# Down projection: all weight sums by accumulating DMA, neighbouring k tiles paired, products reordered, last norms without GpSimd

## The chip, the cores and the metric

The kernel runs on one core of one Trainium2 chip. The metric is the time of one execution on the device in microseconds (us); the median of the runs is compared. Each core has TensorE (PE, matmuls), VectorE (DVE), ScalarE (ACT), GpSimd (POOL) and SyncE (SP, which here only starts transfers), and 16 DMA engines that move data. Each engine works through its own list of instructions in order and waits at semaphores for the others.

## The reference

One encoder layer over two groups of 256 tokens, 1024 channels wide, all in fp32. The part that matters here is the gated feed-forward network at its end, and the norm behind it:

```python
def conv_ffn(x, w_ffn_up, ffn_conv_w, ffn_conv_b, w_ffn_down):
    u = dwconv_centred(x @ w_ffn_up, ffn_conv_w, ffn_conv_b)
    return (jax.nn.gelu(u[..., :D_FF]) * u[..., D_FF:]) @ w_ffn_down
...
    x = layer_norm(DEEPNORM_ALPHA * x + mixed, ln1_g[l], ln1_b[l])
    ff = conv_ffn(x, w_ffn_up[l], ffn_conv_w[l], ffn_conv_b[l], w_ffn_down[l])
    x = layer_norm(DEEPNORM_ALPHA * x + ff, ln2_g[l], ln2_b[l])
```

`D_FF` is 2816, so the product with `w_ffn_down` has 22 k tiles of 128 rows. Its input has 512 rows (4 tiles of 128) and its output 1024 columns (2 halves of 512): 8 output tiles (t, half), each in a PSUM bank of its own.

## The kernel before

Every fp32 matmul is made of three float32r matmuls: each operand is split into a high part (a rounding cast, on ACT) and a low part (a subtraction, on DVE), and high by high, high by low and low by high are added up in PSUM.

The down projection has two parts. The first 8 k tiles are multiplied plainly: `down(f)` for f = 0 to 7 gives 24 matmuls each (L1147 to L1149). The other 14 k tiles form 7 pairs i. For each pair the two k tiles, each cut into a left and a right half of columns, are a 2x2 block matrix `raw[i, r, c]` (tiles named `b...`, 128x512), and the pair's input is a 2x2 block matrix A(i, r, c) of 128x256 blocks. In place of 8 block products the Strassen-Winograd scheme makes 7, on sums of blocks. Product p over all pairs is 7 x 2 x 3 = 42 matmuls (`part`, L1268 to L1270), added up in a pair of banks.

The sums of input blocks (s1 to s4, 128x256) and of weight blocks (t1 to t4, 128x512) are made shortly before or after a product's operands are split. s1 to s4, t1 and t2 are subtractions or additions on DVE (L1168 to L1183). t3 and t4 are `late_sum`: ACT negates the destination (L1187), then a DMA that POOL starts adds the source to it on its way (L1188); POOL itself is occupied only with issuing.

`prepare` makes the split operands (`wop` for weights, `xop` for inputs: cast on ACT in L1222, low part on DVE in L1223), six steps (p, i) ahead of the matmuls. `PRODUCTS` lists for each product the sums to be made before its operands, the operands, the sums to be made after it, and which weight blocks are then free. Its order is the order of work: 1, 5, 6, 3, 7, 2, 4. In the whole program a Tile scheduler decides which order the instructions of an engine finally have.

After the plain part, DVE reads all 8 banks into the residual `y[t][half]` (`residual`, L1052), and the products start the banks anew. Product 2 has banks of its own, product 4 goes on upon the banks of product 7. Each `add_to` (L1262) adds a finished bank to y.

At the end every tile of y is normalised and stored. `layer_norm(..., share=True)` does the first half on DVE (L308, L316) and the second on ACT and GpSimd: ACT standardises it (L324), GpSimd multiplies and adds the gains (L334, L335). The reciprocal root of the variance is a small GpSimd operation (L115) in any case. Row tiles 0 and 1 are normalised while product 4 runs; the last tile is done without sharing, in three pieces.

The weight blocks come by 28 loads of 256 KB each, started by SP (L1156), into slots that are shared with other tiles (62 slots in all); a load waits until its slot is free.

Of the kernel before, what the change touches and what calls it, by code (L numbers as in the profile page):

```python
# [29 lines left out]
NF = DFF // P  # L30
# [13 lines left out]
NP = 7  # L44
# [4 lines left out]
class Encoder:  # L49
# [759 lines left out]
    def build(self):  # L809
        nc, io = self.nc, self.io  # L810
# [51 lines left out]
        with self.tc.manual_schedule(engines=engines):  # L862
# [30 lines left out]
            ps = self.ps("lncol")  # L893
# [138 lines left out]
        y = {}  # L1032
# [18 lines left out]
        def residual(t, h, ps):  # L1051
            nc.vector.scalar_tensor_tensor(y[t][h], y[t][h], ALPHA, ps, op0=ALU.mult, op1=ALU.add)  # L1052
# [27 lines left out]

        hf, hs, up = {}, {}, {}

        def ev_up(f, which):
# [12 lines left out]

# [37 lines left out]

        w_dn = io["w_ffn_down"][0]
        acc = {}
        PL = NF - 2 * NP
        raw, sums, ops = {}, {}, {}
        mm = nc.tensor.matmul
        tt = nc.vector.tensor_tensor  # L1140

        def down_mm(f, t, half, wh, wl):
            down_split(f)
# [6 lines left out]

        def load_pair(i):
            for r in range(2):
                k = PL + r * NP + i
# [4 lines left out]
        def A(i, r, c):  # L1158
            return hf[PL + c * NP + i][:, r * T : r * T + T]

        def S(i):
            if i % 2 == 0 and i // 2 not in sums:
                sums[i // 2] = self.a("ssum")
            return sums[i // 2][:, (i % 2) * T : (i % 2) * T + T]


        def sum_s1(i):
            tt(S(i), A(i, 1, 0), A(i, 1, 1), op=ALU.add)  # L1168

        def sum_s2(i):  # L1170
            tt(S(i), S(i), A(i, 0, 0), op=ALU.subtract)

        def sum_s3(i):
            tt(A(i, 1, 0), A(i, 0, 0), A(i, 1, 0), op=ALU.subtract)
# [22 lines left out]
        PRODUCTS = {  # L1197
            1: ((), lambda i: A(i, 0, 0), lambda i: raw[i, 0, 0], (sum_t1, sum_s1, sum_s3), ()),
            5: ((), S, lambda i: raw[i, 0, 0], (sum_t3,), ()),
            6: ((sum_t2, sum_s2), S, lambda i: raw[i, 0, 0], (sum_t4,), ()),  # L1200
            3: ((sum_s4,), S, lambda i: raw[i, 1, 1], (), ((1, 1),)),
            7: ((), lambda i: A(i, 1, 0), lambda i: raw[i, 0, 1], (), ((0, 1),)),
            2: ((), lambda i: A(i, 0, 1), lambda i: raw[i, 1, 0], (), ((1, 0),)),
            4: ((), lambda i: A(i, 1, 1), lambda i: raw[i, 0, 0], (), ((0, 0),)),
        }
        steps = [(p, i) for p in PRODUCTS for i in range(NP)]
# [3 lines left out]
        def prepare(n):  # L1210
            while len(made) < min(n, len(steps)):
                p, i = next(ahead)
                before, x, w, later, done = PRODUCTS[p]
                for f in before:
                    f(i)
                o = []
                wsrc, xsrc = w(i), x(i)
                wt = self.whl.tile([P, 1024], F32R, tag=("hi", "lo")[len(made) % 2], name="wop")
                xt = self.a("xop", F32R)
                for z, src, n_ in ((wt, wsrc, 512), (xt, xsrc, T)):  # L1220
                    h, l = z[:, :n_], z[:, n_ : 2 * n_]
                    nc.scalar.copy(h, src)  # L1222
                    tt(l, src, h.bitcast(F32), op=ALU.subtract)  # L1223
                    o += [h, l]
                ops[p, i] = o
                for f in later:
                    f(i)
                for r, c in done:
                    del raw[i, r, c]
                if p == 3 and i % 2 == 1 or p == 3 and i == NP - 1:  # L1230
                    del sums[i // 2]
                if p == 7:
                    del hf[PL + i]
                if p == 4:
                    del hf[PL + NP + i]
                made.append((p, i))

        dn = [self.chunk(w_dn, f, 1, 0, D) for f in range(PL)]

        def down(f):  # L1240
            def run():
                if f == 0:
                    for t in range(NTT):
                        for half in range(2):
                            acc[t, half] = self.ps(f"dn{t}{half}", dense=(t >= 2))
                for z in range(f, min(f + 3, PL)):
                    down_split(z)
                wh, wl = dn[f].get()
                for t in range(NTT):
                    for half in range(2):  # L1250
                        down_mm(f, t, half, wh, wl)
# [7 lines left out]
            return run  # L1259

        def add_to(t, half, ps):
            tt(y[t][half], y[t][half], ps, op=ALU.add)  # L1262

        def part(p, i, j, out, first, c=slice(0, 512)):
            wh, wl, xh, xl = ops[p, i]
# [6 lines left out]
        def product(p, bank, first, sinks):  # L1272


            def run():
                n = list(PRODUCTS).index(p) * NP
                for i in range(NP):
                    prepare(n + i + 1 + STEPS)
                    for j in range(2):
                        part(p, i, j, acc[bank[0] + 2 * j, bank[1]], first)  # L1280
                    del ops[p, i]
                for r, c in sinks:
                    for j in range(2):
                        add_to(2 * r + j, c, acc[bank[0] + 2 * j, bank[1]])
            return run

        BA, BB, BC, BD = (0, 0), (1, 0), (0, 1), (1, 1)

        def store(t, h, c=slice(0, 512)):
            nc.sync.dma_start(  # L1290
# [1 line left out]
                y[t][h][:, c],  # L1292
            )

        def tail():
            gb2 = self.gains(io["ln2_g"], io["ln2_b"])
            prepare(len(steps))
            for t in range(2):
                self.layer_norm(y[t], gb2, None, True)
                for h in range(2):  # L1300
                    store(t, h)

            o = acc[BA[0], BA[1]]
            for i in range(NP):
                part(4, i, 0, o, False)
            add_to(2, 0, o)
            self.layer_norm(y[2], gb2, None, True)
            for h in range(2):
                store(2, h)
            st = self.sm([P, 4, 6], "lnst4")  # L1310
            z = y[3]
            for n in range(2):
                c = slice(n * 256, n * 256 + 256)
                nc.vector.bn_stats(st[:, n, :], z[1][:, c])
            for n, bank in enumerate((BC, BD)):
                c = slice(n * 256, n * 256 + 256)
                o = acc[bank][:, c]
# [5 lines left out]
            self.layer_norm(z, gb2, st, False, pieces, lambda h, c: store(3, h, c))  # L1323
# [6 lines left out]
        self.add(product(3, BB, False, [(0, 1)]))  # L1330
        self.add(product(7, BA, False, [(1, 1)]))
        self.add(product(2, BC, True, [(0, 0)]))

        self.add(lambda: add_to(3, 0, acc[BA[0] + 2, BA[1]]))
        self.add(tail)
        self.run_jobs()

# [75 lines left out]
```

## Time and profile before

| | before |
|---|---|
| runs (3) | 945.25 us median, 944.57 to 946.96 |
| the profiled execution | 946.11 us, its span 944.3 us, TensorE clock 0.994 |
| PE busy over the span | 927.4 us (98%) |
| DVE busy | 605.3 us (64%) |
| ACT busy | 407.6 us (43%) |
| POOL busy | 106.5 us (11%) |
| plain part of the down projection | first matmul at 821.21 us, last at 864.50 |
| seven products | 864.73 to 931.8 us |
| last operation of DVE ends | 940.99 us |

Busy time counts work and no waiting. The span is the time from the first to the last instruction; the execution takes 1.81 us more than it. A duration in a row includes the pipeline's fill; the distance of two starts in a row without a wait is what an instruction costs its engine. A note in square brackets at the end of a row is idle time before it and what ended that.

### The profile page before, as it was taken

What the parts mean: (1) busy time and instruction counts of PE and PEld (TensorE: products, weight loads), DVE (VectorE), ACT (ScalarE), POOL (GpSimd) and SP (SyncE); (2) the same over time, 40 slices, a digit from 0 to 9 for tenths busy, and PEclk for the clock granted to TensorE, in tenths of its full rate; (3) what the DMA queues carried; (4) which work ended last, traced back from release to release, by engine and by line L of the source; (5) the groups of instructions that cost most, each with busy time, mean ns of one, the idle gap of its engine ahead of it and who ended that gap; (6) DMA issues with size and microseconds to landing.
All of it is one profiled execution on the core that took longest, in us unless ns stands there. A gap on an engine that the chain in (4) does not pass through costs nothing.

```text
span 944.3 us, 12395 instructions
## 1 busy us (share of the span) xinstructions
PE 927.4 (98%) x4633; PEld 789.3 (84%) x4633; DVE 605.3 (64%) x1145; ACT 407.6 (43%) x761; POOL 106.5 (11%) x105
## 2 busy tenths in 40 slices
PE   8999999999999999999999999999999999999994
PEld 6888888888889998888888889988888888888884
DVE  4584444896777535367667758755555555677997
ACT  4562543434555435344336312533343343454861
POOL 0100100450000000121007401000000000011205
PEclk9999999999999999999999999999999999999998
DMA  8354223224111243433245433333333332473412
GB/s 290 89 161 144 75 68 90 73 62 131 53 46 44 66 136 89 142 96 98 68 123 173 152 89 89 104 98 90 105 96 89 105 96 90 165 228 87 79 45 89
DMA packets 125663, 99.44 MB, mean 105 GB/s; under 512 B 4128, under 2 KB 106532, under 8 KB 125604
## 3 DMA queue, kind: packets, MB, share of 16 engines
q1 hardware_dynamic: 123588, 94.99, 33.2%
q0 software_dynamic: 2016, 3.67, 2.3%
q8 instruction: 36, 0.59, 0.3%
q14 instruction: 23, 0.19, 0.1%
HBM read 92.86 MB, written 2.11 MB: 101 GB/s over the span
## 4 chain that ended last, share of the span: by engine, by line
PE 92%; DVE 3%; POOL 2%; DMA 1%; ACT 1%; issue 0%; POOLq 0%; DVEq 0%; SPq 0%; ACTq 0%
PE ua L122 4%; PE ub L123 4%; PE ub L122 4%; PE ua L123 4%; PE ua L124 4%; PE ub L124 4%; PE vc L837 3%; PE dn L1270 2%; PE dn L1268 2%; PE dn L1269 2%; PE ga L122 2%; PE vog L171 2%; PE vog L172 2%; PE vog L170 2%; PE ga L123 2%; PE ba L122 2%
## 5 line engine op out<-in xcount | busy, mean ns | idle before, releaser
L111 DVE TENSOR_TENSOR wlo<-raw,whi 128x1024 fp32r<-128x1024 f32 (+3 forms) x148 | 176.7, 1198 | 217.2 <-ACT whi L110 217.0
L110 ACT CAST whi<-raw 128x1024 fp32r<-128x1024 f32 (+3 forms) x148 | 148.2, 1009 | 295.7 <-PE ua L123 72.0
L1188 POOL DMA_DIRECT2D b<-b x14 | 12.4, 905 | 293.2 <-ACT xop L1222 270.1
L1270 PE MATMUL dn<-wop,xop 128*128 128x512 f32 (+1 forms) x105 | 39.4, 375 | 0.0
L1269 PE MATMUL dn<-wop,xop 128*128 128x512 f32 (+1 forms) x105 | 39.4, 375 | 0.0
L1268 PE MATMUL dn<-wop,xop 128*128 128x512 f32 (+1 forms) x105 | 39.4, 375 | 0.0
L1223 DVE TENSOR_TENSOR wop<-b,wop 128x512 fp32r<-128x512 f32 x49 | 33.7, 699 | 4.5 <-ACT wop L1222 4.5
L1222 ACT CAST wop<-b 128x512 fp32r<-128x512 f32 x49 | 29.5, 619 | 15.7 <-PE dn L1148 6.0
L405 ACT ACTIVATE prob<-sc,nmax 128x256 f32<-128x256 f32 x48 | 22.4, 475 | 24.7 <-DVE nmax L401 24.6
L1089 ACT ACTIVATE up<-up 128x512 f32<-128x512 f32 x22 | 13.9, 633 | 42.5 <-DVE up L476 42.4
L115 POOL TENSOR_TENSOR rss<-rss,mhalf 128x4 f32<-128x4 f32 (+1 forms) x12 | 22.6, 1884 | 75.5 <-DVE rss L784 75.5
L1269 PEld LDWEIGHTS dn<-wop,xop 128*128 128x128 f32 x105 | 19.8, 188 | 3.6
L1270 PEld LDWEIGHTS dn<-wop,xop 128*128 128x128 f32 x105 | 19.8, 188 | 3.6
L1268 PEld LDWEIGHTS dn<-wop,xop 128*128 128x128 f32 x105 | 19.8, 188 | 3.5
L334 POOL TENSOR_TENSOR y<-y,gain 128x512 f32<-128x512 f32 x11 | 18.4, 1680 | 20.1 <-PE gm L123 19.0
L401 DVE TENSOR_REDUCE nmax<-sc 128x2 f32<-128x512 f32 x24 | 16.4, 683 | 4.3 <-PE sc L124 4.3
L335 POOL TENSOR_TENSOR y<-y,gain 128x512 f32<-128x512 f32 x11 | 18.8, 1716 | 0.5
L115 POOL TENSOR_TENSOR lnmv<-lnmv,mhalf 128x1 f32<-128x1 f32 x8 | 7.7, 959 | 86.9 <-DVE lnmv L297 86.9
L85 DVE TENSOR_TENSOR probTl<-pt,probTh 128x512 fp32r<-128x512 f32 x24 | 16.4, 684 | 1.4 <-ACT probTh L84 1.4
L473 DVE SCALAR_TENSOR_TENSOR up<-ub,col,up 128x510 f32<-128x510 f32 x20 | 14.9, 744 | 2.7 <-ACT up L470 2.7
L996 DVE SCALAR_TENSOR_TENSOR gate<-gate,ba 128x512 f32<-128x512 f32 x8 | 5.5, 686 | 17.1 <-PE ba L124 9.2
L470 ACT ACTIVATE up<-ub,col 128x512 f32<-128x512 f32 x20 | 15.5, 775 | 1.2 <-PE ub L124 1.2
(1371 smaller groups left out, 2933.6 us busy)
## 6 DMA issues: line engine op xcount, KB each, us to landing
raw<-in_w_in SPq DMA_DIRECT2D x48, 512.0 KB
raw<-in_w_ffn_up SPq DMA_DIRECT2D x44, 512.0 KB
b<-in_w_ffn_down SPq DMA_DIRECT2D x28, 256.0 KB
raw<-in_w_mem_kv SPq DMA_DIRECT2D x8, 512.0 KB
raw<-in_w_branch_attn SPq DMA_DIRECT2D x8, 512.0 KB
raw<-in_w_out SPq DMA_DIRECT2D x8, 512.0 KB
raw<-in_w_ffn_down SPq DMA_DIRECT2D x8, 512.0 KB
b<-b POOLq DMA_DIRECT2D x14, 256.0 KB, 3.6
```

The costliest lines, as they stand in the source:

```text
L110: nc.scalar.copy(hi[:, s], raw[:, s])
L111: nc.vector.tensor_tensor(lo[:, s], raw[:, s], hi[:, s].bitcast(F32), op=ALU.subtract)
L115: self.nc.gpsimd.tensor_tensor(out, in_, self.mhalf.to_broadcast(list(in_.shape)), op=ALU.pow)
L122: mm(ps, lh, rh, start=first, stop=False)
L123: mm(ps, lh, rl, start=False, stop=False)
L124: mm(ps, ll, rh, start=False, stop=last)
L837: nc.tensor.matmul(vps[t], memT[2 * c + kk][xi][:, ts], w[wi][:, kk, :], start=(c + kk + xi + wi == 0), stop=(wi == 1 and 2 * c + kk == KT ...
L1222: nc.scalar.copy(h, src)
L1223: tt(l, src, h.bitcast(F32), op=ALU.subtract)
L1268: mm(out, xh[:, ts], wh[:, c], start=first and i == 0, stop=False, skip_group_check=go_on)
L1269: mm(out, xh[:, ts], wl[:, c], start=False, stop=False, skip_group_check=go_on)
L1270: mm(out, xl[:, ts], wh[:, c], start=False, stop=i == NP - 1, skip_group_check=go_on)
```

## The change

- t1 and t2 are made as t3 and t4 are: a negation on ACT and an accumulating DMA from POOL. There are 28 such sums where there were 14.
- A pair is two neighbouring k tiles (8+2i, 9+2i) and no longer tiles 7 apart (8+i, 15+i). s1 and s3 of a pair are made as soon as its second hidden tile is there, in the up projection.
- The products' order is 1, 5, 2, 6, 3, 7, 4. Product 2 goes on upon banks of the plain part; product 4 goes on upon one of the two banks of product 7 and needs new starts for the other output tile only.
- Of the 8 residual reads 4 come after the plain part; the other 4 output tiles get theirs with the first bank that a product adds to them. Within a k tile of the plain part the order of the output tiles is another.
- The last norms share nothing with ACT and GpSimd: both halves are done on DVE. `finish` normalises and stores row tile 0 in product 7 and row tile 1 ahead of product 4; the gains are loaded in product 3.

```diff
         def ev_up(f, which):
...
                 nc.vector.tensor_tensor(hf[f], up[f], u, op=ALU.mult)
+                if f >= PL and (f - PL) % 2:
+                    sum_s1((f - PL) // 2)
+                    sum_s3((f - PL) // 2)
...
-        def sum_t1(i):
-            tt(raw[i, 0, 0], raw[i, 0, 1], raw[i, 0, 0], op=ALU.subtract)
-
-        def sum_t2(i):
-            tt(raw[i, 0, 0], raw[i, 1, 1], raw[i, 0, 0], op=ALU.subtract)
...
+        def sum_t1(i):
+            late_sum(raw[i, 0, 0], raw[i, 0, 1])
+
+        def sum_t2(i):
+            late_sum(raw[i, 0, 0], raw[i, 1, 1])
...
-            1: ((), lambda i: A(i, 0, 0), lambda i: raw[i, 0, 0], (sum_t1, sum_s1, sum_s3), ()),
-            5: ((), S, lambda i: raw[i, 0, 0], (sum_t3,), ()),
-            6: ((sum_t2, sum_s2), S, lambda i: raw[i, 0, 0], (sum_t4,), ()),
+            1: ((), lambda i: A(i, 0, 0), lambda i: raw[i, 0, 0], (sum_t1,), ()),
+            5: ((), S, lambda i: raw[i, 0, 0], (sum_t2, sum_t3), ()),
+            2: ((), lambda i: A(i, 0, 1), lambda i: raw[i, 1, 0], (), ()),
+            6: ((sum_s2,), S, lambda i: raw[i, 0, 0], (sum_t4,), ((1, 0),)),
...
-                        if f == PL - 1:
-                            residual(t, half, acc[t, half])
+                for t, half in ((0, 1), (1, 1), (2, 0), (3, 0), (0, 0), (1, 0), (2, 1), (3, 1)):
+                    down_mm(f, t, half, wh, wl)
+                    if f == PL - 1 and half != t // 2:
+                        add_to(t, half, acc[t, half])
...
+        BA, BB = [acc_of(0, 1), acc_of(1, 1)], [acc_of(2, 0), acc_of(3, 0)]
+        BC, BD = [acc_of(0, 0), acc_of(1, 0)], [acc_of(2, 1), acc_of(3, 1)]
...
+                    if between and i == NP // 2:
+                        between()
...
+        def finish(t, st=None):
+            self.layer_norm(y[t], y["gb2"], st)
+            for h in range(2):
+                store(t, h)
...
-            for t in range(2):
-                self.layer_norm(y[t], gb2, None, True)
...
+            finish(1)
+
+            add_to(3, 0, BA[1]())
+            o = BA[0]()
             for i in range(NP):
                 part(4, i, 0, o, False)
...
+        self.add(product(2, BC, False, [(0, 0)]))
+        self.add(lambda: read(BD, 1, 1))
+        self.add(product(6, BA, False, [(0, 1)]))
+        self.add(product(3, BB, False, [(0, 1)], lambda: y.update(gb2=self.gains(io["ln2_g"], io["ln2_b"]))))
+        self.add(product(7, BA, False, [(1, 1)], lambda: finish(0)))
         self.add(tail)
```

How the lists of the engines change is shown at three places. The weight blocks of one pair carry four numbers; before, those of pair 0 are b_7269, b_7271, b_7273, b_7275 (left upper, right upper, left lower, right lower), now b_7287, b_7289, b_7291, b_7293; pair 1 begins at b_7311 before and b_7329 now, pair 2 at b_7363 and b_7379.

The first place is the plain part, on ACT: the casts of operands (L1222, now L1227), the splits of hidden tiles for the plain matmuls (L84), of plain weights (L110), and the negations (L1187, now L1186). ACT before:

```order
L1222 CAST wop<-b_7311 128x512
L84 CAST hs4h<-hf_5976 128x512
L110 CAST whi<-raw 128x1024
L1187 ACTIVATE b_7313<-b_7313 128x512
L1222 CAST xop<-hf_6341 128x256
L84 CAST hs5h<-hf_6049 128x512
L1222 CAST xop<-hf_6414 128x256
```

ACT now:

```order
L1227 CAST wop<-b_7329 128x512
L1186 ACTIVATE b_7289<-b_7289 128x512
L1186 ACTIVATE b_7329<-b_7329 128x512
L110 CAST whi<-raw 128x1024
L1227 CAST xop<-hf_6417 128x256
L84 CAST hs5h<-hf_6049 128x512
L1186 ACTIVATE b_7331<-b_7331 128x512
L1227 CAST wop<-b_7379 128x512
L1227 CAST xop<-hf_6565 128x256
L84 CAST hs6h<-hf_6122 128x512
L1186 ACTIVATE b_7379<-b_7379 128x512
```

The negation of a pair's right upper block (b_7289, b_7331) must wait until the accumulating DMA that reads it (into b_7287, b_7329) has landed, and the negation of the next pair's left upper block stands behind it.

POOL's accumulating DMAs in the same place, destination and source, before:

```order
L1188 DMA b_7271<-b_7275 128x512
L1188 DMA b_7313<-b_7317 128x512
L1188 DMA b_7365<-b_7369 128x512
L1188 DMA b_7416<-b_7420 128x512
L1188 DMA b_7513<-b_7517 128x512
```

And now:

```order
L1187 DMA b_7287<-b_7289 128x512
L1187 DMA b_7289<-b_7293 128x512
L1187 DMA b_7329<-b_7331 128x512
L1187 DMA b_7331<-b_7335 128x512
L1187 DMA b_7379<-b_7381 128x512
L1187 DMA b_7381<-b_7385 128x512
L1187 DMA b_7429<-b_7431 128x512
L1187 DMA b_7431<-b_7435 128x512
L1187 DMA b_7479<-b_7481 128x512
L1187 DMA b_7523<-b_7525 128x512
L1187 DMA b_7481<-b_7485 128x512
L1187 DMA b_7287<-b_7293 128x512
```

t1 and t3 alternate pair by pair, and t2 (the last row) follows among them; before, only t3 stood here.

The second place is DVE at the end of the plain part: the low parts of operands (L1223, now L1228) and the residual reads (L1052). DVE before:

```order
L1223 TENSOR_TENSOR wop<-b_7553,wop 128x512
L1183 TENSOR_TENSOR b_7269<-b_7275,b_7269 128x512
L1180 TENSOR_TENSOR b_7553<-b_7555,b_7553 128x512
L1223 TENSOR_TENSOR xop<-hf_6633,xop 128x256
L1223 TENSOR_TENSOR xop<-hf_6706,xop 128x256
L1052 SCALAR_TENSOR_TENSOR y_4767<-y_4767,dn_7237 128x512
```

DVE now:

```order
L1228 TENSOR_TENSOR wop<-b_7287,wop 128x512
L1228 TENSOR_TENSOR wop<-b_7563,wop 128x512
L1228 TENSOR_TENSOR wop<-b_7379,wop 128x512
L1228 TENSOR_TENSOR xop<-hf_7011,xop 128x256
L1052 SCALAR_TENSOR_TENSOR y_4768<-y_4768,dn_7256 128x512
L1052 SCALAR_TENSOR_TENSOR y_4778<-y_4778,dn_7258 128x512
L1052 SCALAR_TENSOR_TENSOR y_4787<-y_4787,dn_7259 128x512
L1052 SCALAR_TENSOR_TENSOR y_4797<-y_4797,dn_7261 128x512
L1228 TENSOR_TENSOR wop<-b_7329,wop 128x512
L1228 TENSOR_TENSOR xop<-hf_7153,xop 128x256
```

The input operand of the first product's last pair (hf_7153) stands behind four residual reads; on ACT its cast stands behind the negation of b_7565, which waits for the landing of the last t1.

The third place is DVE at the end: `add_to` (L1262, now L1272), the statistics (L294) and the two halves of the norm's last steps (L308, L316), y_4767 and y_4768 being the halves of row tile 0, y_4777 and y_4778 of tile 1, y_4787 and y_4788 of tile 2, y_4797 and y_4798 of tile 3. DVE before:

```order
L1262 TENSOR_TENSOR y_4767<-y_4767,dn_7238 128x512
L1262 TENSOR_TENSOR y_4777<-y_4777,dn_7242 128x512
L294 BN_STATS lnst<-y_4767 128x6
L294 BN_STATS lnst<-y_4777 128x6
L296 BN_AGGR lnmv<-lnst 128x2
L294 BN_STATS lnst<-y_4778 128x6
L297 TENSOR_SCALAR lnmv<-lnmv 128x1
L308 SCALAR_TENSOR_TENSOR y_4767<-y_4767,lnmv,gain 128x512
L327 SCALAR_TENSOR_TENSOR lnmv<-lnmv 128x1
```

DVE now:

```order
L1228 TENSOR_TENSOR wop<-b_7563,wop 128x512
L1228 TENSOR_TENSOR xop<-hf_7244,xop 128x256
L294 BN_STATS lnst<-y_4777 128x6
L294 BN_STATS lnst<-y_4778 128x6
L1272 TENSOR_TENSOR y_4788<-y_4788,dn_7256 128x512
L1272 TENSOR_TENSOR y_4798<-y_4798,dn_7258 128x512
L296 BN_AGGR lnmv<-lnst 128x2
L1272 TENSOR_TENSOR y_4797<-y_4797,dn_7258 128x512
L297 TENSOR_SCALAR lnmv<-lnmv 128x1
L308 SCALAR_TENSOR_TENSOR y_4777<-y_4777,lnmv,gain 128x512
L308 SCALAR_TENSOR_TENSOR y_4778<-y_4778,lnmv,gain 128x512
```

Before, two norms stand in a row after the last operands; now row tile 0 is finished between the operands, and the reads of product 7's banks (dn_7256, dn_7258) stand here, upon the first of which product 4 goes on.

## Rows read from the trace of the kernel before

**Rows 1.** The page: DVE's busy tenths in 40 slices of the span.

```profile
DVE  4584444896777535367667758755555555677997
```

**Rows 2.** Windows: stretch, length, busy PE, PEld, DVE, ACT, POOL, PEclk, DMA share, GB/s.

```profile
877.00:885.00 8.00, 8.00 (x37) 6.64 (x36) 8.00 (x18) 7.12 (x15) 3.62 (x5) 1.00 0.59 100
```

**Rows 3.** Timeline of PE (start, duration): the products' first and last matmul.

```profile
864.73 0.39 PE L1268 MATMUL dn<-wop,xop 128*128 128x512 f32 x1
...
931.52 0.28 PE L1270 MATMUL dn<-wop,xop 128*128 128x256 f32 x1
```

**Rows 4.** Timeline of DVE, end of the plain part and end of the program.

```profile
859.70 0.76 DVE L1223 TENSOR_TENSOR xop<-hf,xop 128x256 fp32r<-128x256 f32 x2 [2.73 <-ACT xop L1222]
860.38 5.24 DVE L1052 SCALAR_TENSOR_TENSOR y<-y,dn 128x512 f32<-128x512 f32 x8
865.53 0.42 DVE L1168 TENSOR_TENSOR ssum<-hf,hf 128x256 f32<-128x256 f32 x1
865.87 0.69 DVE L1223 TENSOR_TENSOR wop<-b,wop 128x512 fp32r<-128x512 f32 x1
866.47 0.42 DVE L1174 TENSOR_TENSOR hf<-hf 128x256 f32<-128x256 f32 x1
...
936.53 2.48 DVE L308 SCALAR_TENSOR_TENSOR y<-y,lnmv,gain 128x512 f32<-128x512 f32 x2
939.45 1.54 DVE L316 SCALAR_TENSOR_TENSOR y<-y,lnmv,gain 128x256 f32<-128x256 f32 x3 [0.44 <-POOL lnmv L115]
```

**Rows 5.** Groups by line, 740 to 945: count | busy us, mean ns | idle before.

```profile
L308 DVE SCALAR_TENSOR_TENSOR y<-y,lnmv,gain 128x512 f32<-128x512 f32 x5 | 5.0, 1025 | 0.0
...
L316 DVE SCALAR_TENSOR_TENSOR y<-y,lnmv,gain 128x512 f32<-128x512 f32 (+1 forms) x6 | 4.4, 756 | 0.4 <-POOL lnmv L115 0.4
```

**Rows 6.** Waits by line, 800 to 945: us in total, times, longest.

```profile
DVE lnmv L327 <- POOL lnmv L115: 1.3, 3, 0.5
```

**Rows 7.** Accumulating DMAs (issue ns, starts) and their landing: first; a pair; plain part; products.

```profile
L1188 POOL DMA_DIRECT2D b<-b x1: 1065/1065/1065, 828.8 to 828.8; - x1
DMA to landing us min/median/max: 7.0/7.0/7.0
...
L1188 POOL DMA_DIRECT2D b<-b x2: 860/1003/1146, 851.9 to 852.5; - x2
DMA to landing us min/median/max: 3.5/4.5/5.5
...
L1188 POOL DMA_DIRECT2D b<-b x7: 860/867/1146, 828.8 to 859.3; - x7
DMA to landing us min/median/max: 3.2/4.2/7.0
...
L1188 POOL DMA_DIRECT2D b<-b x7: 860/869/937, 873.5 to 889.1; - x7
DMA to landing us min/median/max: 3.3/3.6/4.0
```

**Rows 8.** Timeline of ACT in the plain part.

```profile
827.80 0.63 ACT L1187 ACTIVATE b<-b 128x512 f32<-128x512 f32 x1
828.33 0.39 ACT L1222 CAST xop<-hf 128x256 fp32r<-128x256 f32 x1
...
843.17 1.05 ACT L110 CAST whi<-raw 128x1024 fp32r<-128x1024 f32 x1 [1.68 <-PE dn L1149]
```

**Rows 9.** Timeline of SP: the loads of the paired weight blocks.

```profile
818.46 36.17 SPq L1156 DMA_DIRECT2D b<-in_w_ffn_down  x28
```

**Rows 10.** Windows and timeline of PE at the program's start.

```profile
8.00:12.00 4.00, 3.95 (x14) 3.12 (x14) 2.09 (x6) 1.35 (x7) 0.00 (x0) 0.57 1.03 371
...
8.05 0.77 PE L837 MATMUL vc<-whi,mT00h 128*128 128x512 f32 x1 [2.35 <-ACT whi L110]
9.16 0.63 PE L837 MATMUL vc<-whi,mT00l 128*128 128x512 f32 x1
9.59 0.63 PE L837 MATMUL vc<-whi,mT01l 128*128 128x512 f32 x1
```

More of the change, by code (lines that the diff above doesn't have):

```diff
@@ L1081, in build, with A, S, sum_s1 @@
         hf, hs, up = {}, {}, {}
+        PL = NF - 2 * NP
+        sums = {}
+        tt = nc.vector.tensor_tensor
+        def A(i, r, c):
+            return hf[PL + 2 * i + c][:, r * T : r * T + T]
+        def S(i):
+            if i % 2 == 0 and i // 2 not in sums:
+                sums[i // 2] = self.a("ssum")
+            return sums[i // 2][:, (i % 2) * T : (i % 2) * T + T]
+        def sum_s1(i):
+            tt(S(i), A(i, 1, 0), A(i, 1, 1), op=ALU.add)
+        def sum_s3(i):
+            tt(A(i, 1, 0), A(i, 0, 0), A(i, 1, 0), op=ALU.subtract)
         def ev_up(f, which):
@@ L1136, in build @@
         acc = {}
-        PL = NF - 2 * NP
-        raw, sums, ops = {}, {}, {}
+        raw, ops = {}, {}
         mm = nc.tensor.matmul
-        tt = nc.vector.tensor_tensor
         def down_mm(f, t, half, wh, wl):
@@ L1152, in load_pair @@
             for r in range(2):
-                k = PL + r * NP + i
+                k = PL + 2 * i + r
                 for c in range(2):
@@ L1156, in load_pair @@
                     nc.sync.dma_start(raw[i, r, c], w_dn[k * P : k * P + P, c * 512 : c * 512 + 512])
[L1158 to L1168, printed above, removed]
         def sum_s2(i):
             tt(S(i), S(i), A(i, 0, 0), op=ALU.subtract)
-        def sum_s3(i):
-            tt(A(i, 1, 0), A(i, 0, 0), A(i, 1, 0), op=ALU.subtract)
         def sum_s4(i):
             tt(S(i), A(i, 0, 1), S(i), op=ALU.subtract)
-        def sum_t1(i):
-            tt(raw[i, 0, 0], raw[i, 0, 1], raw[i, 0, 0], op=ALU.subtract)
-        def sum_t2(i):
-            tt(raw[i, 0, 0], raw[i, 1, 1], raw[i, 0, 0], op=ALU.subtract)
         def late_sum(dst, src):
@@ L1232, in prepare, with acc_of @@
                 if p == 7:
-                    del hf[PL + i]
+                    del hf[PL + 2 * i]
                 if p == 4:
-                    del hf[PL + NP + i]
+                    del hf[PL + 2 * i + 1]
                 made.append((p, i))
         dn = [self.chunk(w_dn, f, 1, 0, D) for f in range(PL)]
+        def acc_of(t, half):
+            return lambda: acc[t, half]
         def down(f):
@@ L1248, in run @@
                 wh, wl = dn[f].get()
-                for t in range(NTT):
-                    for half in range(2):
-                        down_mm(f, t, half, wh, wl)
-                        if f == PL - 1:
-                            residual(t, half, acc[t, half])
+                for t, half in ((0, 1), (1, 1), (2, 0), (3, 0), (0, 0), (1, 0), (2, 1), (3, 1)):
+                    down_mm(f, t, half, wh, wl)
+                    if f == PL - 1 and half != t // 2:
+                        add_to(t, half, acc[t, half])
                 del hs[f]
@@ L1259, in down @@
             return run
+        begun = set()
         def add_to(t, half, ps):
-            tt(y[t][half], y[t][half], ps, op=ALU.add)
+            if (t, half) in begun:
+                tt(y[t][half], y[t][half], ps, op=ALU.add)
+            else:
+                residual(t, half, ps)
+                begun.add((t, half))
         def part(p, i, j, out, first, c=slice(0, 512)):
@@ L1270, in part, with read, product @@
             mm(out, xl[:, ts], wh[:, c], start=False, stop=i == NP - 1, skip_group_check=go_on)
-        def product(p, bank, first, sinks):
+        BA, BB = [acc_of(0, 1), acc_of(1, 1)], [acc_of(2, 0), acc_of(3, 0)]
+        BC, BD = [acc_of(0, 0), acc_of(1, 0)], [acc_of(2, 1), acc_of(3, 1)]
+        def read(bank, r, c):
+            for j in range(2):
+                add_to(2 * r + j, c, bank[j]())
+        def product(p, bank, first, sinks, between=None):
             def run():
@@ L1279, in run @@
                     for j in range(2):
-                        part(p, i, j, acc[bank[0] + 2 * j, bank[1]], first)
+                        part(p, i, j, bank[j](), first)
                     del ops[p, i]
+                    if between and i == NP // 2:
+                        between()
                 for r, c in sinks:
-                    for j in range(2):
-                        add_to(2 * r + j, c, acc[bank[0] + 2 * j, bank[1]])
+                    read(bank, r, c)
             return run
-        BA, BB, BC, BD = (0, 0), (1, 0), (0, 1), (1, 1)
         def store(t, h, c=slice(0, 512)):
@@ L1293, in store @@
             )
+        def finish(t, st=None):
+            self.layer_norm(y[t], y["gb2"], st)
+            for h in range(2):
+                store(t, h)
         def tail():
-            gb2 = self.gains(io["ln2_g"], io["ln2_b"])
             prepare(len(steps))
-            for t in range(2):
-                self.layer_norm(y[t], gb2, None, True)
-                for h in range(2):
-                    store(t, h)
-            o = acc[BA[0], BA[1]]
+            finish(1)
+            add_to(3, 0, BA[1]())
+            o = BA[0]()
             for i in range(NP):
                 part(4, i, 0, o, False)
-            add_to(2, 0, o)
[L1307 to L1311, printed above, removed]
+            z = y[3]
+            st = self.sm([P, 4, 6], "lnst4")
+            st2 = self.sm([P, 2, 6], "lnst")
+            nc.vector.bn_stats(st2[:, 1, :], y[2][1])
+            for n in range(2):
+                nc.vector.bn_stats(st[:, n, :], z[1][:, n * 256 : n * 256 + 256])
+            add_to(2, 0, o)
+            nc.vector.bn_stats(st2[:, 0, :], y[2][0])
+            finish(2, st2)
             for n in range(2):
                 c = slice(n * 256, n * 256 + 256)
[L1314 to L1317, printed above, removed]
+                o = BC[n]()[:, c]
                 for i in range(NP):
@@ L1322, in tail @@
             pieces = [(1, slice(0, 512)), (0, slice(0, 256)), (0, slice(256, 512))]
-            self.layer_norm(z, gb2, st, False, pieces, lambda h, c: store(3, h, c))
+            self.layer_norm(z, y["gb2"], st, False, pieces, lambda h, c: store(3, h, c))
         for f in range(PL):
@@ L1328, in build @@
         self.add(product(5, BB, True, [(1, 1)]))
+        self.add(product(2, BC, False, [(0, 0)]))
+        self.add(lambda: read(BD, 1, 1))
         self.add(product(6, BA, False, [(0, 1)]))
[L1330 to L1334, printed above, removed]
+        self.add(product(3, BB, False, [(0, 1)], lambda: y.update(gb2=self.gains(io["ln2_g"], io["ln2_b"]))))
+        self.add(product(7, BA, False, [(1, 1)], lambda: finish(0)))
         self.add(tail)
```

1 line of the change is left out of this document (removed).

## The prediction

> **What bounds the kernel now.** I read the slices first, then the windows of the last 120 us, then the timelines of the engines there. TensorE has no pause in the down projection: the windows show 8.00 us busy in 8.00 at full clock [rows 2], so its matmuls run from 864.73 to 931.52 [rows 3] without a gap that anyone could close: 273 matmuls of 512 columns and 42 of 256 in 66.9 us, 0.227 for a large one if a small one costs half. VectorE is the second engine that is full: after a wait of 2.73 us it goes from its first residual read at 860.38 to its last operation, which starts at 939.45 and takes 1.54, with hardly a pause [rows 4]. So from 860 on two engines set the end together. TensorE's last matmul gives the earliest time at which the last y tile can be finished; VectorE, which works off its list in order, finishes at 940.99, and the last stores end with the span at 944.3, 3.3 us later. A change counts if it makes VectorE's list from 860 on shorter, or if it makes it start later. The number of matmuls is the same in both kernels.
>
> **VectorE's list, counted.** An operation of 128x512 costs it 0.60 us and one of 128x256 0.335 (starts at 865.53, 865.87 and 866.47, [rows 4]). By the lists of instructions, from the first residual read to the end it had 84 of the large, 66 of the small and 11 tiny ones (0.08 each, my estimate from their place in such rows): 50.4 + 22.1 + 0.9 = 73.4 us. The clock on the wall is 940.99 - 860.38 = 80.6, so 7.2 us are waits and stretched operations.
>
> Edit by edit:
>
> - t1 and t2 leave VectorE: 14 x 0.60 = 8.4 us. All of t1 and one t2 stood before 860.38, where VectorE had idle time, and bring nothing there; 6 x 0.60 = 3.6 us stood behind.
> - s1 and s3, 14 x 0.335 = 4.7 us, go to the up projection. VectorE is busy there for 5 to 6 tenths of the slices before the last six [rows 1], so I cost them at nothing. Without that cover they are 4.7 us.
> - Two reads of 128x512 fewer (1.2 us), but the second halves of three norms come to VectorE: 6 x 0.60 = 3.6 us.
> - Together, counted in the new list from its first residual read: 81 large, 65 small, 8 tiny, 71.0 us. VectorE saves 2.4 us of work.
> - GpSimd leaves the norms. What this gives back: three waits for the small root, 1.3 us [rows 6]; 0.4 at the last one, which had to queue behind gain rows [rows 4, 5]; and stretched operations: five L308 took 5.0 us where 0.69 each would be 3.45, and the six L316 4.4 where four large and two small ones take 3.6 [rows 5]; the pair at 936.53 took 2.48 [rows 4]. That is 1.3 + 0.4 + 1.55 + 0.8 = 4.1 us. At worst nothing of the stretch goes, then it is 1.7. I take 4.1, since the stretched ones are those beside GpSimd work.
> - Product 4 now goes on upon a bank of product 7 and so waits until VectorE has read it. From that read on VectorE has 10 large, 2 small and 2 tiny operations, 6.8 us, up to the first half read of the last tile; TensorE starts 0.7 later and has 21 matmuls of 0.227 us and 21 half-size ones ahead of it, 7.2, and 0.28 until the last lands [rows 3]: 8.2. VectorE waits 1.3 us there. Where TensorE gets its bank earlier in VectorE's list it is 0; where another read stands in front, one large operation more, 1.9.
>
> **The chain that decides when VectorE's list starts.** Before, t1 was a VectorE subtraction and only t3 went by DMA; nothing in the plain part hung on a landing. Now, on ScalarE, the negation of a pair's right upper block waits until the DMA of t1 that reads that block has landed, and the casts and the negation for the next pair stand behind it. So landings come in series. An accumulating DMA took 3.2 to 7.0 us from issue to landing, median 4.2 in the plain part; 3.3 to 4.0 among the products; the later of two issued together 5.5, the first of all, beside weight loads, 7.0 [rows 7]. Negations and casts of 128x512 cost 0.53 (starts 827.80, 828.33), a cast of 128x256 0.3, a weight split 1.05 [rows 8]. With 4.2 for single ones:
>
> t1 of pair 0 issued 828.8, landed 835.8. Two negations and POOL's issue of t3 (0.87): pair 1 issued 837.3, landed 841.5. Negation, two casts, a split, negation: pair 2 issued 844.0, landed 848.2. Negation, weight split, cast, negation: pair 3 issued 850.9, landed 855.1. Then POOL issues t3 of pair 3, t1 of pairs 4 and 5 one behind the other; pair 4, issued 856.6, takes the 5.5 of a queued one: 862.1. ScalarE negates three blocks; POOL issues t3 of pair 4, t2 of pair 0, t1 of pair 6, the last at 864.5; the weight loads are over by then, so the longest of the products' landings, 4.0: 868.5. Behind this landing ScalarE does two negations and a cast (1.4), and VectorE can go on with the first product's last input at 870.0; four residual reads and the operands before it are done while it waits. From there 76 large, 64 small and 8 tiny operations: 68.0 us.
>
> **The sum.** Start and work before: 860.4 + 73.4 = 933.8. Now: 870.0 + 68.0 = 938.0. That is 4.2 later; less 4.1 for GpSimd's absence, plus 1.3 for product 4: +1.4 us. Against the profiled execution's 946.11 this is 947.5, and against the median of the runs, 945.25, it is **946.7 us**. The rest of the change I cost at nothing. The 14 further negations (7.4 us) and their issues on POOL fall where ScalarE and POOL have room, except around 877 to 885, where ScalarE is busy 7.12 of 8 [rows 2]; a queue there would cost up to 3. The loads of the paired weights last until 854.6 [rows 9]; 4 sum tiles held longer take the slots of 4 of 28 loads, 36.17/28 x 4 = 5.2 us later, 859.8, while the last pair's t1 is issued at 864.5: hidden, or 1 to 2 us if slots come free late.
>
> **Rivals.**
>
> 1. *The chain is hidden and the kernel is faster.* If landings take the shortest 3.2 [rows 7] and none queues, VectorE's restart comes at 864; work gives 864 + 68.0 = 932.0, 1.8 earlier, and with -4.1 and +1.3 this is -4.6. TensorE allows a little less: product 7 can end at 922.2 (931.8 less 9.6 for product 4), from where VectorE has the 8.2 above, 3.2 to the second half read (4 large, 2 small ones), 3.6 for the last tile and 3.3 to the stores' end: 940.5 against 944.3, -3.8. The time is 941.4. For it: the later landings are 3.3 to 4.0. Against it: the first is 7.0 in a crowd of loads, and all landings but a few of the plain part stand in that crowd. It decides where the restart comes before 865.7. Chance 0.2. The Trainium skill (DMA: Bandwidth & Descriptors, section "Anatomy of one DMA — SWDGE (gpsimd) path") gives 2.0 us plus the bytes over 436,000 per us, 2.6 for these 256 KB; by it this rival would be certain. The trace doesn't agree: not one of 14 landed in under 3.2.
> 2. *The landings slow each other.* Twice as many accumulating DMAs run, and they are issued in twos and threes. If each of five links takes the 5.5 of a queued one, the restart comes at 875 and the sum is +6.4: 951.7. For it: the pair at 851.9 [rows 7], and loads that run on to nearly 860. Against it: the shares fall once the loads are over. It decides from a restart at 871.5 on. Chance 0.25.
> 3. *TensorE pauses and loses its clock.* If VectorE restarts late, operands of the next products or the read in front of product 4 come late, and TensorE stands still for a few us. At the program's start it stood for 2.35 us, and from 8.05 on its clock was at 0.57 and matmuls came every 0.43 us in place of 0.227 [rows 10], at the 1.2 GHz level. Over the about 3.4 us of that stretch it lost 1.7 us by this; so 946.7 + 1.7 = 948.4. The Trainium skill (TensorE: Matmul & The Clock Gate, Part 1) tells of the same two levels, with the low one after idleness. Chance 0.1.
>
> **How the numbers follow.** A change of 0.3% (2.8 us) is about what a measurement of this kernel can tell from none. Forecast 0.45, within it; rival 1, 0.2, faster; rivals 2 and 3, 0.35, slower. So faster 0.2, same 0.45, slower 0.35. The range takes in most of rival 1 and of rival 2: 941.0 to 953.0; the forecast's own is 943.5 to 948.5.
>
> **What would show it.** In the new profile: the starts of t1's DMAs at 837, 844, 851, 857, 864.5, with 4 to 5.5 us to landing; ScalarE's negations waiting for DMA; VectorE idle for several us around 865 to 870 with ScalarE's cast as releaser, then full to the end; no GpSimd work but the root at the end and L308 back at 0.7; a pause of TensorE of about 1 us or more in front of product 4. I am wrong if VectorE restarts before 866 or after 872, if first sums delay the up projection, or if TensorE pauses inside a product.

## The result and the profile after

| | before | after |
|---|---|---|
| median of 5 runs | 944.61 us (943.52 to 946.96) | 950.44 us (949.94 to 952.9) |
| ratio, 95% interval | | 1.0066 [1.0045, 1.0087] |
| span of the profiled execution | 944.3 us | 948.2 us |
| first matmul of the down projection | 821.21 us | 819.20 us |
| last operation of VectorE ends | 940.99 us | 944.55 us |

The change makes the kernel 0.66% slower, 5.8 us between the medians. The forecast was 946.7 with no difference to be told, the range 941.0 to 953.0. The time lies in the range, near the second rival's 951.7, but there is a difference: the kernel is slower by more than the interval, and the time lies outside the forecast's own 943.5 to 948.5.

The two profiled executions differ by 3.9 us, 2.0 less than the part that was changed. Those 2.0 us are from the first microseconds of the program: there TensorE waited 0.84 us for its first weights in the execution of after and 2.35 in that of before, and in before its next matmuls ran at the low clock [rows 10]. From the hundredth matmul (23.99 and 26.07 us) to the down projection the two stay 2.0 to 2.1 us apart. The change touches nothing at that place; the kernels below, all alike there, begin their down projection between 819.25 and 821.47, and one trace of each doesn't show why. So times of the two profiles are compared from the first matmul of the down projection: 2.0 us are added to a time of after to put it beside one of before, and the table of the experiments has a column for it.

ScalarE of the kernel after, timeline of the plain part (start, duration, idle before and what ended it); of its rows only those of negations that waited are shown:

```profile
833.75 1.15 ACT L1186 ACTIVATE b<-b 128x512 f32<-128x512 f32 x2 [5.99 <-DMA b<-b]
839.56 0.63 ACT L1186 ACTIVATE b<-b 128x512 f32<-128x512 f32 x1 [2.89 <-DMA b<-b]
847.94 0.63 ACT L1186 ACTIVATE b<-b 128x512 f32<-128x512 f32 x1 [5.03 <-DMA b<-b]
851.40 0.63 ACT L1186 ACTIVATE b<-b 128x512 f32<-128x512 f32 x1 [1.38 <-DVE wop L1228]
856.98 1.67 ACT L1186 ACTIVATE b<-b 128x512 f32<-128x512 f32 x3 [3.61 <-DMA b<-b]
862.91 2.19 ACT L1186 ACTIVATE b<-b 128x512 f32<-128x512 f32 x4 [3.22 <-DMA b<-b]
870.28 1.15 ACT L1186 ACTIVATE b<-b 128x512 f32<-128x512 f32 x2 [3.29 <-DMA b<-b]
```

Six times the negation of a pair's right upper block waits until the accumulating DMA of the same pair's t1, which reads that block, has landed: 24.0 us in all. There was no such wait before ([rows 8]: the first negation stood at 827.80 without one). POOL's issues in the same stretch (two rows of one t3 each, at 840.50 and 848.87, and the first t1, at 826.74, are left out):

```profile
834.70 1.77 POOL L1187 DMA_DIRECT2D b<-b  x2 [6.89 <-ACT b L1186]
842.39 0.86 POOL L1187 DMA_DIRECT2D b<-b  x1 [1.04 <-ACT xop L1227]
852.34 0.86 POOL L1187 DMA_DIRECT2D b<-b  x1 [2.61 <-ACT xop L1227]
857.91 2.65 POOL L1187 DMA_DIRECT2D b<-b  x3 [4.71 <-ACT b L1186]
863.84 4.46 POOL L1187 DMA_DIRECT2D b<-b  x5 [3.27 <-ACT b L1186]
```

The times from issue to landing, of all 28 accumulating DMAs, of t1 of pair 2 (issued at 842.39), and of the first four of the five issued from 863.84 on:

```profile
DMA to landing us min/median/max: 3.3/4.3/7.0
...
DMA to landing us min/median/max: 5.5/5.5/5.5
...
DMA to landing us min/median/max: 3.4/4.8/6.2
```

The median is about what it was before ([rows 7]: 4.2 in the plain part). What is new is that one waits for the other, and that DMAs issued in a row queue up. The DMA queues of after from 857 to 861, from 861 to 864 and from 864 to 868 (packets, MB, share of the 16 engines; q1 carries the loads, q0 the accumulating DMAs):

```profile
q0 software_dynamic: 156, 0.29, 42.7%
q1 hardware_dynamic: 144, 0.26, 21.6%
...
q0 software_dynamic: 276, 0.50, 97.6%
...
q0 software_dynamic: 254, 0.49, 72.3%
```

From 861 on no load moves any more; the accumulating DMAs have the engines to themselves. VectorE and TensorE after, where the plain part ends:

```profile
865.64 0.69 DVE L1228 TENSOR_TENSOR wop<-b,wop 128x512 fp32r<-128x512 f32 x1 [5.14 <-ACT wop L1227]
...
866.58 2.47 DVE L1052 SCALAR_TENSOR_TENSOR y<-y,dn 128x512 f32<-128x512 f32 x4
...
871.76 0.42 DVE L1228 TENSOR_TENSOR xop<-hf,xop 128x256 fp32r<-128x256 f32 x1 [2.10 <-ACT xop L1227]
...
943.01 1.54 DVE L316 SCALAR_TENSOR_TENSOR y<-y,lnmv,gain 128x256 f32<-128x256 f32 x3
```

```profile
867.32 0.80 PE L1281 MATMUL dn<-wop,xop 128*128 128x512 f32 x1 [4.43 <-DVE y L1052]
867.91 0.63 PE L1282 MATMUL dn<-wop,xop 128*128 128x512 f32 x1
868.33 0.63 PE L1283 MATMUL dn<-wop,xop 128*128 128x512 f32 x1
...
930.15 0.50 PE L1281 MATMUL dn<-wop,xop 128*128 128x512 f32 x1 [2.96 <-DVE y L1272]
```

VectorE stands idle for 5.14 us, then four residual reads (L1052) come at 866.58 where eight came at 860.38 [rows 4]. TensorE's first product must wait for the first of them, 4.43 us, and then runs at 0.43 us per matmul, the 1.2 GHz level (granted clock 0.51 from 867.3 to 870.4), for some 3 us. From 871.76 on VectorE is nearly full to the end (68.59 of 71.00 us busy from 872 to 943); its largest waits there are two for casts of ScalarE, 1.8 us together. In front of product 4 TensorE waits another 2.96 us for VectorE's read.

### The profile page after: what moved, and what is told of

Read it like the earlier page. It is cut to its first block, busy times and chain, and to the rows that moved or that the text cites. A ratio compares the mean times of both kernels' runs of the same rounds, so it can differ in the third digit from the quotient of the medians.

```text
span 948.2 us, 12399 instructions
## 1 busy us (share of the span) xinstructions
PE 929.0 (98%) x4633; PEld 789.6 (83%) x4633; DVE 598.3 (63%) x1132; ACT 410.5 (43%) x772; POOL 110.5 (12%) x113
## 5 line engine op out<-in xcount | busy, mean ns | idle before, releaser
L110 ACT CAST whi<-raw 128x1024 fp32r<-128x1024 f32 (+3 forms) x148 | 148.2, 1009 | 291.8 <-PE ua L123 72.0
L1187 POOL DMA_DIRECT2D b<-b x28 | 24.8, 1046 | 293.0 <-DMA b<-in_w_ffn_down 244.3
L1281 PE MATMUL dn<-wop,xop 128*128 128x512 f32 (+1 forms) x105 | 40.4, 384 | 7.4 <-DVE y L1052 4.4
L1228 DVE TENSOR_TENSOR wop<-b,wop 128x512 fp32r<-128x512 f32 x49 | 33.0, 684 | 13.7 <-ACT wop L1227 13.6
L1282 PE MATMUL dn<-wop,xop 128*128 128x512 f32 (+1 forms) x105 | 40.0, 381 | 0.0
L1283 PE MATMUL dn<-wop,xop 128*128 128x512 f32 (+1 forms) x105 | 39.8, 380 | 0.0
L1227 ACT CAST wop<-b 128x512 fp32r<-128x512 f32 x49 | 29.2, 616 | 1.9 <-PE dn L1283 1.1
L1186 ACT ACTIVATE b<-b 128x512 f32<-128x512 f32 x28 | 16.7, 625 | 27.6 <-DMA b<-b 24.0
L334 POOL TENSOR_TENSOR y<-y,gain 128x512 f32<-128x512 f32 x8 | 14.5, 1827 | 18.1 <-ACT y L324 18.1
L996 DVE SCALAR_TENSOR_TENSOR gate<-gate,ba 128x512 f32<-128x512 f32 x8 | 5.5, 685 | 17.2 <-PE ba L124 9.3
```

The lines of the kernel that those rows point to most:

```text
L110: nc.scalar.copy(hi[:, s], raw[:, s])
L1281: mm(out, xh[:, ts], wh[:, c], start=first and i == 0, stop=False, skip_group_check=go_on)
```

## The experiments

Theory A: t1 by DMA turns the plain part into a series of landings, VectorE's list begins late, and since it is full to the end, the end is late. Theory B: the doubled DMA traffic slows itself and the loads. Theory C: the loss is in the new end, with the norms on VectorE and product 4 behind a read. Medians in one table (ratios to before, with their 95% intervals; before's own median was 945.78 in the first four, 945.85 in the last four). The last column is the profiled execution from the first matmul of the down projection to its end; for before it is 123.1 us, for after 129.0. It leaves out the program's start. Runs of one kernel can differ by 2 us (with t1 and t2 on VectorE four took 941.5 to 942.2 and four 943.2 to 943.5), so differences of 1 or 2 us between two of these medians mean little where the last column doesn't show them.

| kernel | median us | ratio | down projection to end, us |
|---|---|---|---|
| after, t1 on VectorE | 941.86 | 0.9964 [0.9950, 0.9977] | 120.4 |
| after, t2 on VectorE | 949.96 | 1.0054 [1.0039, 1.0069] | 128.3 |
| after, t1 and t2 on VectorE | 942.65 | 0.9970 [0.9960, 0.9981] | 120.6 |
| after, t1 by DMA from HBM | 943.77 | 0.9980 [0.9969, 0.9991] | 120.7 |
| before, t1 and t2 by DMA | 961.10 | 1.0163 [1.0142, 1.0183] | 140.3 |
| before, norms all on VectorE | 943.99 | 0.9983 [0.9974, 0.9992] | 121.4 |
| after, product 4 on a free bank | 951.78 | 1.0061 [1.0048, 1.0075] | 129.1 |
| after, t1 on VectorE, product 4 on a free bank | 943.23 | 0.9976 [0.9964, 0.9987] | 120.7 |

**t1 back on VectorE.**

```diff
         def sum_t1(i):
-            late_sum(raw[i, 0, 0], raw[i, 0, 1])
+            tt(raw[i, 0, 0], raw[i, 0, 1], raw[i, 0, 0], op=ALU.subtract)
```

> The changed kernel with the seven t1 sums back on VectorE (t2 stays an accumulating DMA). Theory A (series of landings: the negation of a pair's right upper block waits for t1's landing, everything behind it on ScalarE and so VectorE's list start late): the negations no longer wait for a landing in the plain part, VectorE starts its residual reads near the end of the plain part's first banks as before, the 4.4 us pause in front of the first product is gone, and the time falls below before to about 941 to 942 (rival 1's sum). Theory B (traffic: 28 accumulating DMAs slow each other and the loads): a quarter of them is gone, so about a quarter to a half of the 5.8 us, 947.5 to 949. Theory C (the loss is in the new end: norms on VectorE, product 4 behind product 7's read): 950, the second pause of 3.0 us stays as it is.

941.86: theory A's number. Seven of the 28 DMAs made 8.6 us between the medians, and as much from the first matmul of the down projection on (129.0 to 120.4). The timeline of VectorE in this kernel (its down projection begins at 819.56):

```profile
858.75 0.69 DVE L1228 TENSOR_TENSOR wop<-b,wop 128x512 fp32r<-128x512 f32 x1 [1.21 <-ACT wop L1227]
...
859.70 2.47 DVE L1052 SCALAR_TENSOR_TENSOR y<-y,dn 128x512 f32<-128x512 f32 x4
...
863.76 0.42 DVE L1228 TENSOR_TENSOR xop<-hf,xop 128x256 fp32r<-128x256 f32 x1 [0.99 <-ACT xop L1227]
...
935.12 1.54 DVE L316 SCALAR_TENSOR_TENSOR y<-y,lnmv,gain 128x256 f32<-128x256 f32 x3
```

By the clocks of the two profiles, whose down projections begin within 0.4 us, the residual reads begin 6.9 us earlier than after, the first product's last input comes at 863.76 in place of 871.76, and no wait of a negation for an accumulating DMA is left; TensorE has no pause in front of the first product. VectorE ends 7.9 us earlier. Theory C is out too: the new end is still there, TensorE still waits 1.1 us in front of product 4, and the kernel is faster than before.

**t2 back on VectorE.**

```diff
         def sum_t2(i):
-            late_sum(raw[i, 0, 0], raw[i, 1, 1])
+            tt(raw[i, 0, 0], raw[i, 1, 1], raw[i, 0, 0], op=ALU.subtract)
```

> The changed kernel with the seven t2 sums back on VectorE (t1 stays an accumulating DMA). Theory A: the series of t1 landings stays, only one t2 issue in front of the last t1 goes (about 1 us earlier), and VectorE gets 7 x 0.60 = 4.2 us more behind its late start: 951 to 954, slower than the changed kernel. Theory B: as many DMAs gone as with t1 on VectorE, so the same 947.5 to 949. Theory C: 950 to 954.

949.96, like the changed kernel. The traffic is as small as with t1 on VectorE, and nothing is gained: B is wrong in its size. But A had expected a loss of 1 to 4 us, which didn't come. Three of the t2 sums fall into waits of VectorE, one at 860.07 and two in its wait for the last t1, and the first product's last input follows at once:

```profile
869.16 0.68 DVE L1228 TENSOR_TENSOR wop<-b,wop 128x512 fp32r<-128x512 f32 x1
869.76 1.28 DVE L1193 TENSOR_TENSOR b<-b,b 128x512 f32<-128x512 f32 x2
871.11 0.42 DVE L1228 TENSOR_TENSOR xop<-hf,xop 128x256 fp32r<-128x256 f32 x1
```

So 1.8 us of the 4.2 were free, that input came 0.65 earlier, and VectorE was busy for 70.30 of the 71.00 us from 872 to 943, against 68.59 after: the rest filled small waits. Those were the waits for ScalarE's casts, 1.8 us after and 0.5 here, where ScalarE has seven negations fewer.

**Both on VectorE**, the two edits above together.

> The changed kernel with t1 and t2 on VectorE, as before; left of the change are the pairing of neighbours with first sums in the up projection, the product order, the reads and the norms. Theory A: no landing in the plain part is waited for; VectorE carries 4.2 us more than with t1 alone on it, of which part is hidden: 942 to 945.5. Theory B: the traffic is that of before: 944 to 945. Theory C: the pause in front of product 4 stays and the time is 949 or more.

942.65, in A's range. What is left of the change (pairing, order, reads, norms) is worth 3.1 us by the medians (945.78 - 942.65), 2.5 by the last column. From t2 by DMA there is nothing to be told: 941.86 and 942.65 are 0.8 apart, the runs overlap (941.65 to 942.26, 941.54 to 943.49), and the last column has 120.4 and 120.6.

**t1 by DMA, but from HBM.** The same amount is moved; the source is the weight where it came from, so no negation has to wait until it has been read.

```diff
         def sum_t1(i):
-            late_sum(raw[i, 0, 0], raw[i, 0, 1])
+            k = PL + 2 * i
+            late_sum(raw[i, 0, 0], w_dn[k * P : k * P + P, 512:1024])
```

> The changed kernel, t1 still an accumulating DMA of the same size, but its source is the weight in HBM instead of the right upper block in SBUF. So nothing waits for t1's landing before that block is negated; traffic is not less than in the changed kernel (1.8 MB more are read from HBM). Theory A: the series is broken: 941 to 945. Theory B: no better than the changed kernel, 950 or more. Theory C: 950.

943.77, A again, and the cleanest of the four: 28 accumulating DMAs as in the changed kernel, with the negations of t1 still on ScalarE, and the DMAs land later. Those issued between 820 and 870, by source, with their times to landing:

```profile
L1187 POOL DMA_DIRECT2D b<-b x13: 860/872/1296, 828.9 to 869.5; - x13
L1187 POOL DMA_DIRECT2D b<-in_w_ffn_down x7: 868/1172/1927, 828.1 to 856.1; - x7
DMA to landing us min/median/max: 3.3/5.8/8.4
```

And VectorE's residual reads in its timeline:

```profile
861.11 2.47 DVE L1052 SCALAR_TENSOR_TENSOR y<-y,dn 128x512 f32<-128x512 f32 x4
```

With slower transfers and more traffic VectorE's reads begin at 861.11 all the same (its down projection at 820.59). It is the wait of one on the other that costs, not the transfer by itself; how long each transfer takes counts only where the next one waits for it.

**Before, with the DMA sums alone.** In the kernel before, the same two edits the other way round (t1 and t2 as `late_sum`).

> The kernel before with one part of the change alone: t1 and t2 by accumulating DMA. Theory A (series of t1 landings): ScalarE waits for landings in the plain part as in the changed kernel, VectorE's last operands in front of the residual reads come at about 870 to 872 in place of 859.7, TensorE pauses in front of the first product, and VectorE's list, 3.6 us shorter, ends 6 to 8 us later: 950 to 954. Theory C (the loss is in order, pairing and norms): 944 to 946.

961.10, more than A had expected: 15.3 us (17.2 by the last column, whose execution was the slowest of the four). The mechanism is A's, in its waits:

```profile
ACT b L1187 <- DMA b<-b: 29.3, 6, 7.0
...
PE dn L1268 <- DVE y L1052: 13.5, 2, 12.8
```

Negations wait 29.3 us for landings (24.0 in the changed kernel), all eight residual reads come at 877.20, and TensorE stands 12.8 us in front of the first product. The expectation had VectorE go on at 872 at the latest; the series is longer here, and the list behind it has eight reads where the changed kernel has four. The whole change, which has the same two sums beside its other edits, loses only 5.8.

**Before, with the norms alone.**

```diff
-                self.layer_norm(y[t], gb2, None, True)
+                self.layer_norm(y[t], gb2, None, False)
...
-            self.layer_norm(y[2], gb2, None, True)
+            self.layer_norm(y[2], gb2, None, False)
```

> The kernel before with one other part alone: the last three norms that shared work with ScalarE and GpSimd done wholly on VectorE. By the prediction's terms VectorE gets 3.6 us of work and loses 4.1 us of waits and stretch: -0.5, so 944 to 946. If GpSimd's stretch of VectorE's operations is not its doing, it is +1.9: 947.

943.99, 1.9 us faster (945.85 - 943.99; 1.7 by the last column) though VectorE has six large operations more. The groups of the two steps of the norm in this kernel:

```profile
L316 DVE SCALAR_TENSOR_TENSOR y<-y,lnmv,gain 128x512 f32<-128x512 f32 (+1 forms) x9 | 5.8, 687 | 0.0
L308 DVE SCALAR_TENSOR_TENSOR y<-y,lnmv,gain 128x512 f32<-128x512 f32 x8 | 5.6, 744 | 0.0
```

Against 1025 and 756 ns a piece before [rows 5]: eight now take little more than five did. The long ones before were those beside GpSimd's gain rows: of the five L308 the two with no gain row beside them took 741 and 745 ns, the other three 806, 1089 and 1746.

**Product 4 on a free bank.**

```diff
-            o = BA[0]()
+            add_to(2, 0, BA[0]())
+            o = BD[0]()
             for i in range(NP):
-                part(4, i, 0, o, False)
+                part(4, i, 0, o, True)
```

> The changed kernel with product 4's first half on a bank that is long free, in place of product 7's bank (one VectorE addition more, 0.6 us). The 3.0 us pause of TensorE in front of product 4 goes. Theory A (VectorE's late list sets the end): no gain, 949.5 to 951. Rival D (this pause of TensorE is on the path): 947.5 to 948.5.

951.78, 0.8 above A's range: no gain. The 2.96 us pause is gone, TensorE begins its last matmul at 935.92 in place of 939.12, and the end is where it was, or up to 0.6 later for the addition. TensorE's second pause was not on the path; VectorE's list was. From its restart at 871.97 to its end VectorE does not wait for TensorE once in this kernel, though TensorE's first pause (4.34 us) is still there: that pause doesn't set the end either.

**Both, t1 on VectorE and the free bank.**

> Both: t1 on VectorE and product 4 on a free bank. With t1 on VectorE TensorE still waited 1.1 us in front of product 4. If TensorE sets the end there, 1.1 less is gained and 0.6 given back on VectorE: 941.0 to 941.9, not to be told from 941.86; if VectorE does, 942.5.

943.23, 1.4 us above the kernel with t1 on VectorE alone. Most of that is not the edit's: the down projection began at 821.47 in this profile and at 819.56 in the other, and from there the two took 120.7 and 120.4. So the free bank brings nothing here, as if VectorE set the end. The changed kernel with t1 on VectorE has the best median, 941.86, 3.9 us faster than before and 8.6 than after; from the down projection on, all four versions in which no negation waits for t1 are within 0.3 us of each other and 2.4 to 2.7 faster than before.

## Why the prediction was right or wrong

- *The call of no difference*: wrong. Slower had a chance of 0.35. That the time lies in the range is owed to the range's width, which took in most of rival 2. By its own sign, a restart of VectorE after 872, the prediction was wrong on the chain: in before's time it came at 873.8.
- *VectorE's list from the restart on*: right in its sum. 68.0 us of work and 4.4 of waits were forecast (7.2 - 4.1 + 1.3), 72.4; from 871.76 to 944.55 it took 72.8. Its parts are in part luck: product 4 made VectorE wait 0.26 and not 1.3, and ScalarE's casts, costed at nothing, 1.8.
- *GpSimd leaves the norms, 4.1 us for 3.6 of work*: right in direction, small in size. -0.5 was forecast, -1.9 was measured with that part alone. About 1 us of the difference is one small operation of the shared norm, L327, costed at 0.08: of its three, one took 1.24 us in the trace of before.
- *First sums in the up projection, at nothing*: right. The two profiles stay 2.0 to 2.1 us apart from the hundredth matmul to the down projection.
- *The chain of landings decides when VectorE's list starts*: right, shown by taking it away in two ways.
- *Its end at 870.0*: this is the term that was mis-sized. It came at 873.8 (871.76 + 2.0), 3.8 us late. Link by link, in before's time: pair 1 was issued at 837.3 as forecast (835.3); pair 2 at 844.4 for 844.0, but its landing took 5.5 and not 4.2. Pair 3 was issued at 854.3 for 850.9, since ScalarE's negation waited for VectorE's low part behind the weight split as well (1.38 us, the row at 851.40), a wait that the hand-made chain left out; its landing took 4.6 for 4.2. Pair 4's landing took 4.4 where 5.5 had been taken, which won 1.1 back. The last t1 was issued at 866.9 for 864.5, and its landing took 5.3 where 4.0 was taken, the longest of the landings among the products in the kernel before. The loads were over by then, as forecast: the last was begun 41.1 us after the first, 859.6 for the forecast's 859.8, and none moved after 861 (863 in before's time). The 5.3 is the queue's: this t1 was the third of four issued within 1.7 us from 863.84 on. So of the 3.8 us the five landings made 2.1 (24.2 for 22.1), the wait left out 1.4.
- *Four residual reads are done while VectorE waits*: true of VectorE, but the step forgot that TensorE's first product waits for those reads. They came at 866.58 behind an operand that hung on the same chain, and TensorE stood for 4.43 us.
- *Product 4, VectorE waits 1.3 us*: wrong way round. VectorE waited 0.26, TensorE 2.96, because VectorE was the late one. It cost nothing, as the free bank shows.
- *Rival 1*: not one of 28 landings took less than 3.3 us. Its time, 941.4, was all but reached (941.86) where no negation waits for t1.
- *Rival 2*: its time, 951.7, was nearest, and its reason holds in part. VectorE's restart went past its point of 871.5, and the chain's landings took 2.1 us more than forecast, where the rival had all five at 5.5, 5.4 more; one of them by queueing behind other accumulating DMAs, as the rival said. The median of all 28 landings (4.3) doesn't show this, because few of them are in the chain. The wait for VectorE's low part is not in the rival.
- *Rival 3* came true as a mechanism: a pause and then 0.43 us per matmul from 867.91 to about 870.5. The lost 1.6 us (8 x 0.2) are covered: with product 4 on a free bank the pause was still there and VectorE did not wait for TensorE afterwards.

The sum thus becomes: +1.4 forecast, +3.8 for the chain, +0.4 for VectorE's list, +0.3 for the last store (3.65 after VectorE's end, not 3.3): +5.9, where the two profiles differ by 5.9 and the medians by 5.8.

## What to carry to other kernels

An accumulating DMA frees an engine of an addition but puts its landing, 3 to 7 us, where 0.6 us stood, and any in-order engine that must overwrite the source waits for it with all that stands behind. Of several that are issued in a row, the later ones land later. Before moving a sum to a DMA, look for the next writer of its source and its place in that engine's list; here a source that nobody overwrites, or leaving one sum of four on an engine with idle time, turned 0.66% slower into 0.2% to 0.4% faster. When two engines are full to the end, remove waits of the one whose list starts late; the other's pauses may cost nothing.

## What the runs showed that was not expected

- Four accumulating DMAs issued 0.55 us apart landed one after the other, 3.4, 4.3, 5.3 and 6.2 us after their issue: each took 0.9 to 1.0 us longer than the one before it.
- From HBM the seven accumulating DMAs of 256 KB took 5.2 to 7.5 us, and cost less than those from SBUF, because no negation waited for them. Others beside them, from SBUF, took up to 8.4.
- GpSimd's gain rows cost VectorE more than doing that work itself: eight norm steps (L308) took 5.6 us without the gain rows where five had taken 5.0 with them.
